# Two more raw weight buffers, one hi and one lo tile fewer, and the first chunk's transposes issued later, in a float32 hybrid layer

## The chip, the cores and the metric

The kernel runs on one core of a Trainium2 chip. The metric is the device time of one execution in microseconds (us). Five engines work in parallel, each in the order of its own queue: TensorE (PE) with its weight loads (PEld), VectorE (DVE), ScalarE (ACT), GpSimd (POOL) and SyncE (SP). SP issues nearly all of the DMA transfers here.

## The reference, cut to what matters

One decoder layer over 272 positions (16 meta tokens and 256 tokens) with a model width of 2048. The part that the change touches is its feed-forward half, on the 256 tokens:

```python
u = rmsnorm(h, attn_norm_w[l]);  proj = u @ w_in[l]           # 2048 x 7184
# ... differential attention (8 heads) and gated DeltaNet (8 heads) on the columns of proj
h = h + jnp.concatenate([o_a, o_d], axis=-1) @ w_out[l]
u = rmsnorm(h, ffn_norm_w[l])
h = h + (jax.nn.silu(u @ w_gate[l]) * (u @ w_up[l])) @ w_down[l]
return h[:, LEAD:]                                             # the 256 tokens
```

FFN_HIDDEN is 5632. All inputs and outputs are float32.

## The kernel before, in words

**Products in three parts.** A float32 weight tile is split into a high part `hi` (ACT rounds the raw tile, L274) and a low part `lo` (DVE subtracts, L275). The left sides are split likewise (`uh`, `ul`; `hT` has both parts in one tile). A product is hi\*hi, hi\*lo and lo\*hi, three matmuls of 128x512 on PE (L1381 in the stages in question, L1199 before).

**Weights as one stream.** The list `order` holds all transfers in the order of use, 512 KB each: w_in, w_out, then for the first 512 columns of the hidden layer (chunk 0) w_gate and w_up one after the other, then for chunks 1 to 10 (`NCH` is 11) pairs of a gate and an up tile, then w_down in two passes of 1024 output columns, with pairs of tiles. A raw tile goes through three steps:

- `load_to` (L261) issues its transfer into a buffer of the ring `raw`;
- `split_to` makes `hi` and `lo` from it;
- `next_w` hands these to the products, and before that asks for the split of the tiles ahead and for the loads ahead of those.

The rings have `WR` = 4 raw buffers, and `WS` = 4 tiles of `hi` and of `lo`, with `WS2` = 2 more of each once the feed-forward stage has opened a pool of its own (`more`): six.

**Plain pairs and groups.** In chunks 1 to 10 there are 8 pairs of weight tiles each (q = 0 to 7), in a pass of w_down 22. A plain pair is two w tiles of 12 matmuls. At the q in `SEVEN` (2, 4, 6) and `DSEVEN` (7, 9, 11, 13, 15, 17, 19) a pair is multiplied in Strassen's manner, seven products in place of eight: the group has four weight tiles, named by their kinds g (6 matmuls), u (3), t (6) and s (6), 21 in all. g and u come from the two raw tiles; t and s are sums of both, made by DVE (L291 to L294) in a ring of two `sum` buffers when g is split. A raw buffer is free again when the last of these has read it: L275's `lo` of the tile, as a rule.

**Who sets the order.** ACT and SP take their instructions in the order in which the code is written (`PINNED`). PE's and DVE's order is set by a scheduler when the program is built, so it shifts when buffers or steps change. Work beside the products (`tasks`) is written as generators; the products call `tasks.step()` after each part, and a `yield n` resumes after n steps.

**Chunk 0.** Gate and up columns of the first chunk are streamed one after the other (`stream`); `ffn_task` then multiplies them on DVE (L1306, `gact`), and after a `yield` `to_hT` transposes the result on PE (L1277), copies it out on ACT (L1292) and makes its low part on DVE (L1293). At that time PE already works on chunk 1, whose first products are in the other set of PSUM banks (`aux`).

**The down product.** Pass 1 makes columns 0 to 1023, pass 2 the rest; each ends with additions to the residual (L1516) and stores (L1518). The residual comes back by L1484.

Of the kernel before, what the change touches and what calls it, by code (L numbers as in the profile page):

```python
# [8 lines left out]
F32 = mybir.dt.float32  # L9
# [6 lines left out]
P = 128  # L16
# [13 lines left out]
KC = (0, 72, 144, T)  # L30
R1, R2 = 12, 10
WR, WS = 4, 4
WS2 = 2
WHOLE = 8
SEVEN = (2, 4, 6)
DSEVEN = (7, 9, 11, 13, 15, 17, 19)
# [130 lines left out]
def layer(tc, xT, aw, x, w_in, w_ba, w_out, w_gate, w_up, w_down, cmask, dist, par, out):  # L167
# [3 lines left out]
    def pool(name, bufs=1, space=None):  # L171
        cm = tc.tile_pool(name=name, bufs=bufs, **({"space": space} if space else {}))
        return cm, cm.__enter__()
# [8 lines left out]
    cm_w, wp = pool("wp")  # L182
# [21 lines left out]
    def act(out_, in_, func, **kw):  # L204

        act_table("silu_and_others" if func == AF.Silu else "natural_log_exp_and_others")
        S.activation(out_, in_, func, **kw)
# [4 lines left out]
    def at_least(k, n):  # L212
        return lambda: done.get(k, 0) >= n
# [39 lines left out]
    pos = [0, 0, 0, 0]  # L253
    more = []

    def load_to(n, parts=1, eng=nc.sync):
        while pos[0] < min(n, len(order)):
            src, a, b = order[pos[0]]
            raw = wp.tile([P, a, b], F32, tag="raw", bufs=WR, name=f"raw{pos[0]}")
            for i in range(0, a, a // parts):  # L260
                eng.dma_start(out=raw[:, i:i + a // parts], in_=src[:, i:i + a // parts])  # L261
            raws[pos[0]] = raw
            pos[0] += 1

    def split(raw, n, a, b, parts=1, rows=slice(0, None)):

        k = n % (WS + WS2) if more else 0
        if k < WS:
            hi, lo = (wp.tile([P, a, b], F32R, tag=t, bufs=WS, name=f"{t}{n}") for t in ("hi", "lo"))
        else:  # L270
            hi, lo = (more[0].tile([P, a, b], F32R, tag=f"{t}2", bufs=WS2, name=f"{t}{n}") for t in ("hi", "lo"))
        for j in range(0, a, a // parts):
# [5 lines left out]
    def split_to(n, parts=1):  # L278
        while pos[1] < min(n, len(forms)):
            m = pos[1]  # L280
            kind, i = forms[m]
            load_to(i + (1 if kind == "w" else 2))
            src, a, b = order[i]
            if kind == "w":
                ready[m] = split(raws.pop(i), m, a, b, parts)
                pos[3] += 1
            elif kind == "g":
                g, u = raws[i], raws[i + 1]
                ready[m] = split(g, m, a, b)
                t, s = (more[0].tile([P, 2, 512], F32, tag="sum", bufs=2, name=f"{n}{i}") for n in "ts")  # L290
                V.tensor_tensor(t[:, 0], u[:, 0], g[:, 0], ALU.subtract)  # L291
                V.tensor_tensor(t[:, 1], u[:, 1], u[:, 0], ALU.subtract)  # L292
                V.tensor_tensor(s[:, 0], u[:, 1], t[:, 0], ALU.subtract)  # L293
                V.tensor_tensor(s[:, 1], g[:, 1], s[:, 0], ALU.subtract)  # L294
                sums_["t"], sums_["s"] = t, s
            elif kind == "u":
                raws.pop(i)
                ready[m] = split(raws.pop(i + 1), m, a, b, rows=slice(1, 2))
                pos[3] += 2
            else:  # L300
                ready[m] = split(sums_[kind], m, a, b)
            pos[1] += 1

    def next_w():
        i = pos[2]
        pos[2] += 1
        split_to(i + WS + (WS2 if more else 0))
        load_to(pos[3] + WR - 1)
        return ready.pop(i)


# [3 lines left out]
    nc.sync.dma_start(out=xr[0][:, 0:1, :], in_=xT[:, 0:1, :])  # L315
    nc.sync.dma_start(out=aw_sb, in_=aw)
    load_to(1, 2, S)

    act_table("natural_log_exp_and_others")
# [820 lines left out]
    def proj(t0):  # L1140

        tasks.until(lambda: mm.live <= 2)
        acc = [mm.now(), mm.now()]
        n = T - t0
        for q in range(4):
            hi, lo = next_w()
            for k in range(4):
                kt = 4 * q + k
                for c in range(2):
                    cs = slice(c * P, (c + 1) * P)  # L1150
                    for i, (a, b) in enumerate(((hi, xh), (hi, xl), (lo, xh))):
                        PE.matmul(acc[c][:, 0:n], a[:, k, cs], b[:, kt, t0:T],  # L1152
                                  start=(kt == 0 and i == 0), stop=(kt == KT - 1 and i == 2))
                tasks.step()
        return acc
# [29 lines left out]
    def stream(kts, lhs, need=None, acc=None, last=True, ring=mm):  # L1185

        first = acc is None
        if first:
            tasks.until(lambda: ring.live <= 2)
            acc = [ring.now(), ring.now()]  # L1190
        for i, kt in enumerate(kts):
            if i % 2 == 0:
                hi, lo = next_w()
            if need:
                tasks.until(need(kt))
            for b in range(2):
                ah, al = lhs(kt, b)
                for j, (l, r) in enumerate(((ah, hi), (ah, lo), (al, hi))):
                    PE.matmul(acc[b], l, r[:, i % 2, :], start=(first and i == 0 and j == 0),  # L1199
                              stop=(last and i == len(kts) - 1 and j == 2))  # L1200
            tasks.step()
            tasks.step()
        return acc
# [68 lines left out]
    def to_hT(c, b, h_):  # L1272

        ring = rings[c % 2]
        pst = yield from ring.get(4, P)
        for j in range(4):
            PE.transpose(pst[:, j, :], h_[:, P * j:P * (j + 1)], ident)  # L1277
        fpool[1].free()
        yield 1
        if c not in hT:  # L1280
            n = f"hT{c}"
            if c < 4:
                hT[c] = bigp.tile([P, 2, 4, SEQ], F32R, tag="big", name=n)
            elif c < 7:
                hT[c] = keep.tile([P, 2, 4, SEQ], F32R, tag=("v_c", "k_c", "q_c")[c - 4], name=n)
            elif c < WHOLE:
                hT[c] = fpool[0].tile([P, 2, 4, SEQ], F32R, tag=n, name=n)
            else:
                hT[c] = fpool[0].tile([P, 4, SEQ], F32, tag=n, name=n)
        bs = slice(P * b, P * (b + 1))  # L1290
        if c < WHOLE:
            S.copy(hT[c][:, 0, :, bs], pst)  # L1292
            V.tensor_tensor(hT[c][:, 1, :, bs], pst, hT[c][:, 0, :, bs], ALU.subtract)  # L1293
        else:
            S.copy(hT[c][:, :, bs], pst)
        ring.free()
        mark(f"hT{c}")

    def ffn_task(c, b, pg, pu):
        g_ = yield from fpool[1].get(512)  # L1300
        act(g_, pg, AF.Silu, scale=rr[:, b:b + 1])
        mm.free()
        yield at_least(f"up{c}", 1)
        yield 1
        ps = pu[b]
        V.scalar_tensor_tensor(g_, ps, rr[:, b:b + 1], g_, ALU.mult, ALU.mult)  # L1306
        mm.free()
        yield 2
        yield from to_hT(c, b, g_)


# [55 lines left out]
    def block(c, name, nq, seven, lhs, need, mid, end):  # L1367
# [15 lines left out]
        for q in range(nq):  # L1383
            k = 2 * q
            if need:
                tasks.until(need(k))
            if q not in seven:
                for col in range(2):
                    hi, lo = next_w()
                    for i in range(2):  # L1390
                        for b in range(2):
                            product(("x", 2 * col + b), lhs(k + i, b), (hi[:, i], lo[:, i]))
                            tasks.step()
                    if q == nq - 1:
                        end(col, x)
                continue
            if not y:
                tasks.until(lambda: other.live == 0)
                y += [other.now() for _ in range(4)]
            tasks.until(at_least(f"side{(name, q)}", 1))  # L1400
            s1, s2_, s3, s4 = sides[name, q]
            plan = (((("y", 0), lhs(k, 0), 0), (("x", 0), lhs(k + 1, 0), 1)), ((("x", 2), s4, 1),),
                    ((("y", 3), s1, 0), (("y", 2), s3, 1)), ((("y", 1), s2_, 0), (("x", 1), lhs(k + 1, 1), 1)))
            for part in plan:
                hi, lo = next_w()
                for bank, a, i in part:
                    product(bank, a, (hi[:, i], lo[:, i]))
                    tasks.step()
            if q == seven[-1]:
                mid(y)  # L1410
# [32 lines left out]
    for b in range(2):  # L1443
        tasks.spawn(ffn_task(0, b, pg[b], pu), urgent=True)
# [180 lines left out]
```

## Time and profile before

| | |
|---|---|
| median of 3 runs | 1223.23 us (1222.27 to 1226.79) |
| profiled execution | 1224.38 us, of which the trace's span is 1222.6 us |
| PE busy | 1209.2 us, 7316 matmuls |
| DVE, ACT busy | 983.6 and 692.3 us |
| DMA | 228.54 MB, mean 187 GB/s, 57.4% of the 16 engines' time on the queue of SP |
| granted TensorE clock | 1.00 |

Times within the span: chunk 0's up columns end at about 557 us, chunks 1 to 10 run to 984.2, pass 1 of the down product to 1099.1, pass 2 to 1218. A matmul of 128x512 has a duration of 0.39 us in the trace, but the next one starts 0.227 us after it, since they are pipelined. So PE is lost only where two starts lie further apart, and its busy share is near 100% even where it barely keeps up.

### The profile page before, as it was taken

The numbers are of one execution on the slowest core, as the hardware profiler recorded it, in microseconds if no ns is written. First come the engines' busy times: TensorE is split into PE (matmuls) and PEld (weight loads), VectorE is DVE, ScalarE is ACT, GpSimd is POOL, SyncE is SP. The second block draws the span as 40 slices with busy tenths as digits, with TensorE's granted clock in tenths as the row PEclk, the third lists the DMA queues.
The fourth block names the chain that finished last, engine by engine and source line by source line (L and its number), as shares of the span: only waits on it lengthen the run. The fifth ranks groups of instructions, "written<-read, shape, count | busy, mean of one in ns | idle before, by whom it ended". The sixth has DMA issues, their size and how long they took to land.

```text
span 1222.6 us, 19223 instructions
## 1 busy us (share of the span) xinstructions
PE 1209.2 (99%) x7316; PEld 1060.0 (87%) x7316; DVE 983.6 (80%) x1573; ACT 692.3 (57%) x1087; POOL 6.1 (0%) x14
## 2 busy tenths in 40 slices
PE   9999999999999999999999999999999999999998
PEld 7999999999999988887888888888888888888876
DVE  7989974686676666668889988998998899886686
ACT  7674465275776665455555556555555665553552
POOL 0000000000000000000000000000000000000000
PEclk9999999999999999999999999999999999999999
DMA  8466564344544645685665665566566565567543
GB/s 293 124 207 195 145 187 121 112 124 145 172 140 139 229 162 178 191 277 167 196 206 186 195 218 190 192 204 217 166 208 216 187 211 197 201 225 276 181 164 133
DMA packets 151869, 228.54 MB, mean 187 GB/s; under 512 B 11736, under 2 KB 72672, under 8 KB 151264
## 3 DMA queue, kind: packets, MB, share of 16 engines
q1 hardware_dynamic: 151232, 226.78, 57.4%
q8 instruction: 57, 0.93, 0.3%
q10 hardware_dynamic: 544, 0.52, 0.1%
q14 instruction: 36, 0.29, 0.1%
HBM read 221.83 MB, written 5.45 MB: 186 GB/s over the span
## 4 chain that ended last, share of the span: by engine, by line
PE 85%; DVE 7%; DMA 4%; ACT 2%; issue 1%; SPq 0%; DVEq 0%; ACTq 0%
PE aux L1381 25%; PE mm L1152 23%; PE mm L1381 21%; PE mm L1199 10%; DVE lo L275 3%; DMA raw<-in_w_down_dram 3%; ACT hi L274 1%; PE aux L1100 1%; PE aux L1055 1%; DMA raw<-in_w_in_dram 0%; PE mm L1277 0%; DVE s L293 0%; DMA raw<-in_w_up_dram 0%; DVE r L581 0%; PE aux L1277 0%
## 5 line engine op out<-in xcount | busy, mean ns | idle before, releaser
L274 ACT CAST hi<-raw 128x1024 fp32r<-128x1024 f32 (+1 forms) x412 | 405.1, 996 | 325.0 <-PE mm L1152 93.3
L275 DVE TENSOR_TENSOR lo<-raw,hi 128x1024 fp32r<-128x1024 f32 (+1 forms) x412 | 470.6, 1153 | 141.6 <-ACT hi L274 139.1
L1152 PE MATMUL mm<-xh,hi 128*128 128x272 f32 (+2 forms) x896 | 258.4, 289 | 0.0
L1152 PE MATMUL mm<-xl,hi 128*128 128x272 f32 (+2 forms) x896 | 255.9, 286 | 0.9 <-DVE xl L384 0.6
L1152 PE MATMUL mm<-xh,lo 128*128 128x272 f32 (+2 forms) x896 | 255.0, 286 | 1.0 <-DVE lo L275 1.0
L1152 PEld LDWEIGHTS mm<-xl,hi 128*128 128x128 f32 x896 | 168.5, 188 | 2.2 <-DVE xl L384 2.0
L1152 PEld LDWEIGHTS mm<-xh,hi 128*128 128x128 f32 x896 | 168.6, 188 | 2.1 <-issue 1.5
L1152 PEld LDWEIGHTS mm<-xh,lo 128*128 128x128 f32 x896 | 168.2, 188 | 1.6 <-DVE lo L275 1.4
L1381 PE MATMUL aux<-hi,uh 128*128 128x512 f32 x260 | 101.6, 391 | 0.0
L1381 PE MATMUL mm<-hi,uh 128*128 128x512 f32 x260 | 101.6, 391 | 0.0
L1381 PE MATMUL aux<-hi,ul 128*128 128x512 f32 x260 | 101.3, 390 | 0.0
L1381 PE MATMUL mm<-hi,ul 128*128 128x512 f32 x260 | 101.2, 389 | 0.0
L1381 PE MATMUL aux<-lo,uh 128*128 128x512 f32 x260 | 101.2, 389 | 0.0
L1381 PE MATMUL mm<-lo,uh 128*128 128x512 f32 x260 | 101.2, 389 | 0.0
L1381 PE MATMUL aux<-hi,hT 128*128 128x512 f32 x216 | 70.2, 389 | 0.0
L1381 PE MATMUL mm<-hi,hT 128*128 128x512 f32 x216 | 70.0, 389 | 0.0
L274 ACT CAST hi<-s 128x1024 fp32r<-128x1024 f32 x44 | 46.3, 1053 | 38.0 <-DVE s L294 34.5
L291 DVE TENSOR_TENSOR t<-raw,raw 128x512 f32<-128x512 f32 x44 | 30.2, 687 | 38.7 <-DMA raw<-in_w_down_dram 25.2
L274 ACT CAST hi<-t 128x1024 fp32r<-128x1024 f32 x44 | 46.3, 1053 | 26.2 <-DVE t L292 11.3
L1381 PEld LDWEIGHTS aux<-hi,ul 128*128 128x128 f32 x260 | 48.8, 188 | 10.2
L1381 PEld LDWEIGHTS mm<-hi,ul 128*128 128x128 f32 x260 | 48.8, 188 | 10.2
L1381 PEld LDWEIGHTS mm<-hi,uh 128*128 128x128 f32 x260 | 48.8, 188 | 10.0
(418 smaller groups left out, 2046.8 us busy)
## 6 DMA issues: line engine op xcount, KB each, us to landing
raw<-in_w_in_dram SPq DMA_DIRECT2D x111, 512.0 KB, 3.6
raw<-in_w_gate_dram SPq DMA_DIRECT2D x88, 512.0 KB, 3.7
raw<-in_w_up_dram SPq DMA_DIRECT2D x88, 512.0 KB, 4.4
raw<-in_w_down_dram SPq DMA_DIRECT2D x88, 512.0 KB, 4.6
raw<-in_w_out_dram SPq DMA_DIRECT2D x32, 512.0 KB, 4.2
x<-x1d SPq DMA_DIRECT2D x8, 256.0 KB, 4.8
xr<-in_xT_dram SPq DMA_DIRECT2D x7, 272.0 KB, 5.8
out_dram<-x SPq DMA_DIRECT2D x6, 256.0 KB, 5.1
```

The source lines that it names most:

```text
L274: S.copy(hi[:, js], raw[:, js])
L275: V.tensor_tensor(lo[:, js], raw[:, js], hi[:, js], ALU.subtract)
L291: V.tensor_tensor(t[:, 0], u[:, 0], g[:, 0], ALU.subtract)
L1055: PE.matmul(pss[m][:, cut[n]], q[ms, P * n:P * (n + 1)], k[ms, 0:NK[n]], start=True, stop=True)
L1100: PE.matmul(po[:, n, :], l, r, start=(j == 0), stop=(j == 1 + n))
L1152: PE.matmul(acc[c][:, 0:n], a[:, k, cs], b[:, kt, t0:T], start=(kt == 0 and i == 0), stop=(kt == KT - 1 and i == 2))
L1199: PE.matmul(acc[b], l, r[:, i % 2, :], start=(first and i == 0 and j == 0), stop=(last and i == len(kts) - 1 and j == 2))
L1381: PE.matmul((x if bank[0] == "x" else y)[bank[1]], l, r, start=first, stop=todo[bank] == 0)
```

## The change

The raw ring gets two more buffers, from the pool of the feed-forward stage, so six raws can be loaded or waiting. The rings of `hi` and `lo` lose one tile each there, so five tiles can be ahead of PE and not six. Bytes of SBUF stay the same: two raw tiles of 512 KB come, one `hi` and one `lo` of 512 KB go. And `ffn_task`, which runs for chunk 0 alone, waits eight steps and not two between the multiplication and the transposes.

```diff
-WS2 = 2
+WS2, WR2 = 1, 2
...
     def load_to(n, parts=1, eng=nc.sync):
         while pos[0] < min(n, len(order)):
             src, a, b = order[pos[0]]
-            raw = wp.tile([P, a, b], F32, tag="raw", bufs=WR, name=f"raw{pos[0]}")
+            if more and pos[0] % (WR + WR2) >= WR:
+                raw = more[0].tile([P, a, b], F32, tag="raw2", bufs=WR2, name=f"raw{pos[0]}")
+            else:
+                raw = wp.tile([P, a, b], F32, tag="raw", bufs=WR, name=f"raw{pos[0]}")
...
         split_to(i + WS + (WS2 if more else 0))
-        load_to(pos[3] + WR - 1)
+        load_to(pos[3] + WR + (WR2 if more else 0) - 1)
...
     def ffn_task(c, b, pg, pu):
...
-        yield 2
+        yield 8
         yield from to_hT(c, b, g_)
```

Lines after L259 move by three in the changed kernel: L275 becomes L278, L291 L294, L1277 L1280, L1306 L1309, L1381 L1384.

What stands on PE at the end of chunk 0, before; `aux` are products of chunk 1, and `mm<-ident,gact` are the transposes, four in a row for each half of the tokens:

```order
L1381 MATMUL aux_6787<-hi_6674,uh 128x512
L1381 MATMUL aux_6787<-lo_6675,uh 128x512
L1381 MATMUL aux_6787<-hi_6674,ul 128x512
L1277 MATMUL mm_6813<-ident,gact_6609 128x128 x4
L1381 MATMUL aux_6788<-hi_6674,uh 128x512
L1381 MATMUL aux_6788<-lo_6675,uh 128x512
L1277 MATMUL mm_6818<-ident,gact_6612 128x128 x4
L1381 MATMUL aux_6788<-hi_6674,ul 128x512
```

And now, from the same product (`hi` 6674 is 6690 here):

```order
L1384 MATMUL aux_6781<-hi_6690,ul 128x512
L1384 MATMUL aux_6782<-hi_6690,uh 128x512
L1384 MATMUL aux_6782<-lo_6691,uh 128x512
L1384 MATMUL aux_6782<-hi_6690,ul 128x512
L1384 MATMUL aux_6779<-hi_6714,uh 128x512
L1384 MATMUL aux_6779<-lo_6715,uh 128x512
L1384 MATMUL aux_6779<-hi_6714,ul 128x512
L1384 MATMUL aux_6780<-hi_6714,uh 128x512
L1384 MATMUL aux_6780<-lo_6715,uh 128x512
L1384 MATMUL aux_6780<-hi_6714,ul 128x512
L1280 MATMUL mm_6841<-ident,gact_6607 128x128 x4
L1280 MATMUL mm_6846<-ident,gact_6610 128x128 x4
```

The first four transposes have moved behind nine more products, and the second four stand directly behind them.

What stands on DVE in pass 2 of the down product, before, from the t tile of one group to the u tile of the next. The number in a name (`raw394`, `lo473`) counts raw and split tiles through the program: 472 and 473 are the t and s of a group, 474 and 475 the plain pair behind it, 476 and 477 the g and u of the next group, and t394 and s394 that group's sums:

```order
L275 TENSOR_TENSOR lo472_11875<-t390_11851,hi472_11874 128x1024
L275 TENSOR_TENSOR lo473_11885<-s390_11852,hi473_11884 128x1024
L275 TENSOR_TENSOR lo474_11901<-raw392_11839,hi474_11900 128x1024
L291 TENSOR_TENSOR t394_11934<-raw395_11904,raw394_11866 128x512
L292 TENSOR_TENSOR t394_11934<-raw395_11904 128x512
L293 TENSOR_TENSOR s394_11935<-raw395_11904,t394_11934 128x512
L275 TENSOR_TENSOR lo475_11919<-raw393_11864,hi475_11918 128x1024
L294 TENSOR_TENSOR s394_11935<-raw394_11866,s394_11935 128x512
L275 TENSOR_TENSOR lo476_11931<-raw394_11866,hi476_11930 128x1024
L275 TENSOR_TENSOR lo477_11944<-raw395_11904,hi477_11943 128x512
```

And now, in the same place:

```order
L278 TENSOR_TENSOR lo472_11885<-t390_11858,hi472_11884 128x1024
L294 TENSOR_TENSOR t394_11941<-raw395_11874,raw394_11849 128x512
L295 TENSOR_TENSOR t394_11941<-raw395_11874 128x512
L278 TENSOR_TENSOR lo473_11901<-s390_11859,hi473_11900 128x1024
L296 TENSOR_TENSOR s394_11942<-raw395_11874,t394_11941 128x512
L297 TENSOR_TENSOR s394_11942<-raw394_11849,s394_11942 128x512
L278 TENSOR_TENSOR lo474_11917<-raw392_11793,hi474_11916 128x1024
L278 TENSOR_TENSOR lo475_11929<-raw393_11837,hi475_11928 128x1024
L278 TENSOR_TENSOR lo476_11938<-raw394_11849,hi476_11937 128x1024
L278 TENSOR_TENSOR lo477_11954<-raw395_11874,hi477_11953 128x512
```

The sums t394 and s394, which read raw395, the last raw tile of the next group, have moved ahead of `lo` of s (473) and of both plain tiles (474, 475). With four raws, raw395 takes the buffer of raw391; with six, that of raw389. In pass 1 DVE's order changes in the same way from the sums of the group at q = 13 on; those of q = 9 and 11 stay behind `lo` of their g tile.

## The prediction

> **What bounds the kernel now.** I read the engines' shares first, then the busy time by stage, then what ended PE's idle time, then the chain of waits where PE stalls.
>
> ```profile
> PE 1209.2 (99%) x7316; PEld 1060.0 (87%) x7316; DVE 983.6 (80%) x1573; ACT 692.3 (57%) x1087; POOL 6.1 (0%) x14
> ```
>
> PE is busy in all but 13.4 of 1222.6 us, and the change removes no matmul. So it can give back only idle time of PE in the stages that it touches: chunk 0's end, chunks 1 to 10, and the two passes of the down product.
>
> ```profile
> 555.00:600.00 45.00, 43.66 (x198) 35.87 (x197) 39.38 (x56) 24.36 (x29) 0.00 (x0) 1.00 0.54 173
> 600.00:984.20 384.20, 384.20 (x1733) 318.84 (x1732) 347.84 (x414) 219.01 (x244) 0.00 (x0) 1.00 0.61 199
> 984.20:1099.10 114.90, 114.90 (x513) 95.22 (x512) 106.26 (x152) 66.55 (x80) 0.00 (x0) 1.00 0.61 206
> 1099.10:1218.00 118.90, 115.64 (x508) 94.73 (x506) 85.47 (x98) 52.71 (x54) 0.00 (x0) 1.00 0.56 190
> ```
>
> The columns are the stretch, its length, then busy time of PE, weight loads, DVE, ACT and POOL, the granted clock (1.00 throughout), DMA share and GB/s. PE loses 1.34 us at chunk 0's end and 3.3 us in down pass 2 (from 1099.1); in the chunks and in pass 1 it loses nothing. DVE, at 347.84 of 384.20 us, is nearly as full as PE.
>
> The loss at chunk 0, on PE and then on DVE:
>
> ```profile
> 562.36 0.39 PE L1381 MATMUL aux<-hi,ul 128*128 128x512 f32 x1
> 564.08 0.66 PE L1277 MATMUL mm<-ident,gact 128*128 128x128 f32 x4 [1.34 <-DVE gact L1306]
> ```
>
> ```profile
> 563.29 0.74 DVE L1306 SCALAR_TENSOR_TENSOR gact<-mm,rr,gact 128x512 f32<-128x512 f32 x1
> ...
> 564.15 0.74 DVE L1306 SCALAR_TENSOR_TENSOR gact<-mm,rr,gact 128x512 f32<-128x512 f32 x1
> ```
>
> The transposes stand 1.72 us behind the matmul before them, because DVE writes gact late. The loss in pass 2, by periods of one plain pair of weight tiles and one Strassen-like group (12 + 12 + 21 = 45 matmuls), L1381's matmuls only:
>
> ```profile
> 1157.57:1167.77 10.20, 10.20 (x46) 8.45 (x45) 1.00 0.54 191
> 1167.77:1178.84 11.07, 10.54 (x47) 8.37 (x45) 1.00 0.53 176
> 1178.84:1190.27 11.43, 10.50 (x46) 8.37 (x45) 1.00 0.53 183
> 1190.27:1202.57 12.30, 10.51 (x46) 8.37 (x45) 1.00 0.53 174
> ```
>
> An undisturbed period is 10.20 us, 0.2267 per matmul: 2.72 for a plain tile, 4.76 for a group. The last three exceed it by 0.87 + 1.23 + 2.10 = 4.2 us. The chain of waits there:
>
> ```profile
> 1166.62 6.34 DMA raw<-in_w_down_dram
> ...
> 1178.48 5.95 DMA raw<-in_w_down_dram
> ...
> 1189.95 6.77 DMA raw<-in_w_down_dram
> ```
>
> These starts are 11.86 and 11.47 us apart: a loop of load and DVE, longer than PE's period, uses up the lead and then stalls PE. DVE in one turn of it:
>
> ```profile
> 1173.09 0.69 DVE L291 TENSOR_TENSOR t<-raw,raw 128x512 f32<-128x512 f32 x1 [3.08 <-DMA raw<-in_w_down_dram]
> 1173.69 0.68 DVE L292 TENSOR_TENSOR t<-raw 128x512 f32<-128x512 f32 x1
> 1174.30 0.69 DVE L293 TENSOR_TENSOR s<-raw,t 128x512 f32<-128x512 f32 x1
> 1174.90 1.22 DVE L275 TENSOR_TENSOR lo<-raw,hi 128x1024 fp32r<-128x1024 f32 x1
> 1176.04 0.68 DVE L294 TENSOR_TENSOR s<-raw,s 128x512 f32<-128x512 f32 x1
> 1176.64 1.82 DVE L275 TENSOR_TENSOR lo<-raw,hi 128x1024 fp32r<-128x1024 f32 x2
> 1178.38 1.22 DVE L275 TENSOR_TENSOR lo<-t,hi 128x1024 fp32r<-128x1024 f32 x1
> ```
>
> The first sum t of the next group waits 3.08 us for its second raw tile (u), and the lo that PE wants next stands behind it in DVE's queue (1174.90). That u could only be requested when lo of the old u had freed its buffer, 4 raws back.
>
> **The change part by part.**
>
> *Transposes.* They move behind 9 more matmuls, to 562.36 + 10 x 0.2267 = 564.6. The first gact is done at 563.29 + 0.74 = 564.03, the second at 564.89, when the second four come up (four take some 0.45 in a row, by the 0.66 of the row above less one's drain: about 565.05). Both fit even with DVE unmoved, and DVE's new order puts the gact ahead of one lo (1.13). Removed: 1.72 - 0.23 = 1.5 us. The copies out of the transposes come about 2 us later against PE's work; the next products in those banks come 18 matmuls on, 4.1 us. Bounds: 0 (the wait moves along) to -1.5; I take -1.5.
>
> *Six raws.* They remove no load and add none. u's buffer is now that of the raw six earlier, the second plain tile of the pair before, so the request can leave half a period sooner. But DVE's new order in the deep part of both passes uses that up: t of the next group now stands ahead of lo of s of this group. One turn becomes: t, t, lo s, s, s, lo of plain tile a, lo of plain tile b; b's end frees u's buffer. By the pitches above (0.60 for a sum, 1.13 for a lo, 1.22 for the last) a's lo ends 0.6 + 0.6 + 1.13 + 0.6 + 0.6 + 1.22 = 4.8 after t starts, and b's 1.15 later. Then u is the second load of a burst of four. What a second load takes, bounded by the nearest rows:
>
> ```profile
> 1139.87 0.37 SPq L261 DMA_DIRECT2D raw<-in_w_down_dram  x1
> 1141.00 0.37 SPq L261 DMA_DIRECT2D raw<-in_w_down_dram  x1
> 1026.39 0.37 SPq L261 DMA_DIRECT2D raw<-in_w_down_dram  x1
> 1027.53 0.37 SPq L261 DMA_DIRECT2D raw<-in_w_down_dram  x1
> 1177.88 0.37 SPq L261 DMA_DIRECT2D raw<-in_w_down_dram  x1
> ```
>
> ```profile
> raw<-in_w_down_dram SPq DMA_DIRECT2D x1, 512.0 KB, 3.6
> raw<-in_w_down_dram SPq DMA_DIRECT2D x1, 512.0 KB, 6.2
> raw<-in_w_down_dram SPq DMA_DIRECT2D x1, 512.0 KB, 3.5
> raw<-in_w_down_dram SPq DMA_DIRECT2D x1, 512.0 KB, 5.0
> raw<-in_w_down_dram SPq DMA_DIRECT2D x1, 512.0 KB, 5.2
> ```
>
> The second fence has the us to landing, in the same order: firsts of a burst 3.6 and 3.5, their seconds 6.2 and 5.0, and 5.2 for the second of another burst. The burst at 1139.87 is spaced as the new one will be and has the 6.2; 1027.53 also came 1.14 after a first and has 5.0. I take their middle, 5.6. The new turn is L = 4.8 + 1.15 + 5.6 = 11.5 us (10.95 to 12.15): no shorter than the 11.5 to 11.9 of now, and above 10.20.
>
> *Rings of five.* A cast waits until PE has left the tile five back:
>
> ```profile
> 676.62 1.05 ACT L274 CAST hi<-raw 128x1024 fp32r<-128x1024 f32 x1 [1.67 <-PE aux L1381]
> ```
>
> Cast 1.05, lo 1.22 and two handovers make 2.5 us from PE's release to a finished lo (about 0.2 for the handovers is my estimate). The tightest tile is the plain one behind a group: between its release and its use PE has only the group's 4.76 us, where a sixth tile gave 2.72 more. Its slack falls from 5.0 to 2.3 us.
>
> *Pass 2*, counted from its start: PE has 7 plain pairs ahead (38.1 us), so lo of tile a of q8 is done at 38.1 + 2.5 = 40.6; from there one turn per group, five turns to a of q18: 40.6 + 5 L = 98.1. PE wants it at 12 pairs and 6 groups, 65.3 + 28.6 = 93.9, and its lo one matmul later, 94.1. Lost: 4.0 us (1.3 to 7.3), against 4.2 now: -0.2.
>
> *Pass 1*: DVE keeps the old order for the first three groups, whose raws come early; the new one begins behind group 11. Tile a of q12 is done at 9 pairs + 2 groups + 2.5 = 61.0; three turns later, 61.0 + 3 L = 95.5 against 94.1: +1.4 us (0 to 3.4), where nothing is lost now.
>
> *Chunks.* Only one t per chunk (that of q6) has the late request, and pairs 7, 0 and 1 follow, in which DVE catches up. Slack 2.3 less 11.5 - 10.2 leaves 1.0: no cost taken; where L exceeds 12.5, the excess in each of ten chunks.
>
> The moved x1 loads and output stores (two raws now stand ahead of the x1 loads on SP) fall in the plain pairs that open a pass, with 7 pairs of work in hand: nothing.
>
> Sum: -1.5 - 0.2 + 1.4 = -0.3 us. The profiled execution took 1224.38 us (span 1222.6), 1.15 above the median of 1223.23; the difference is set against the median: 1222.9, say 1223.0.
>
> **The rivals.**
>
> *B, the loads keep ahead.* If the second load landed 4.3 us after its request, L would be 10.25 and all stalls would go: -1.5 - 4.2 = -5.7, 1217.5. For it speaks a close pair in the chunks, whose second load landed after 4.3 us:
>
> ```profile
> 661.50 0.37 SPq L261 DMA_DIRECT2D raw<-in_w_gate_dram  x1
> 662.10 0.37 SPq L261 DMA_DIRECT2D raw<-in_w_up_dram  x1
> ```
>
> ```profile
> raw<-in_w_up_dram SPq DMA_DIRECT2D x1, 512.0 KB, 4.3
> ```
>
> The two are 0.6 us apart. Against it stand the three seconds of the down product. The Trainium skill, SBUF — State Buffer, "The DMA setup-cost knee", prices a transfer at about 2 us plus its bytes over 436 GB/s, which makes an estimate of 3.2 us here; by that L would be 9.2 and the outcome this rival's. The trace agrees for a first load (3.6) and not for a second.
>
> *C, the shallower rings and the late load decide.* If a second load takes 6.4 us or more, L is 12.4: pass 1 loses 61.0 + 37.2 - 94.1 = 4.1, pass 2 40.6 + 62.0 - 94.1 = 8.5, together with the transposes -1.5 + 4.1 + 8.5 - 4.2 = +6.9: 1230. From there each chunk adds its excess too. The row of 6.2 is near; 5.0 and 5.2 are not.
>
> *D, only the transposes fail*: the gact moves back with them, and the sum is +1.2: 1224.5.
>
> **How the numbers follow.** 0.5% is 6.1 us, about what a measurement can tell from no change: 1217.1 to 1229.3 is "same". My forecast has 0.64 (own range 1218.5 to 1228.3, from L = 10.95: -1.5 - 2.9 + 0 = -4.4, and L = 12.15: -1.5 + 3.1 + 3.4 = +5.0). B 0.18, of which 0.04 beyond 1217.1; C 0.10, of which 0.08 above 1229.3; D 0.08. Faster 0.04, same 0.88, slower 0.08. The range takes in B and the upper end of L: 1217.5 to 1228.5.
>
> **What would show it.** No gap before L1280's transposes in chunk 0. In both passes t (L294) idles for a raw of w_down and lo of s stands behind it; turns of 11 to 12 us; PE gaps of 0.5 to 1.5 us at lo of plain tile a of q14 to q18, in pass 1 as well. ACT's waits on PE grow in the chunks while PE keeps its 100%. I am wrong if a second load lands in under 4.5 us (no gaps) or over 6.4 (gaps in the chunks), or if DVE's queue runs so far ahead that t's wait falls before anything is due.

## The result

The changed kernel takes 1229.28 us (median of 7 runs, 1228.21 to 1230.45), the kernel before, run beside it, 1224.82 us (7 runs, 1222.27 to 1226.79). The ratio is 1.0042 (95% interval 1.0032 to 1.0052): slower by about 4.5 us. The forecast was 1223.0, a gain of 0.3 us within a range of 1217.5 to 1228.5.

The same four stretches as before, in the changed kernel's profile (execution 1228.59 us, span 1226.8): chunk 0's end, chunks 1 to 10, pass 1, pass 2. The columns are those of the prediction's table; the second row begins at the first matmul of chunk 1 and overlaps the first.

```profile
555.00:600.00 45.00, 45.00 (x204) 37.33 (x203) 40.07 (x57) 25.89 (x33) 0.00 (x0) 1.00 0.55 180
559.30:983.20 423.90, 423.90 (x1911) 351.92 (x1911) 382.46 (x459) 242.65 (x272) 0.00 (x0) 1.00 0.60 197
983.20:1102.10 118.90, 116.98 (x516) 95.70 (x515) 108.19 (x154) 66.09 (x79) 0.00 (x0) 1.00 0.61 207
1102.10:1222.60 120.50, 116.99 (x508) 94.46 (x506) 86.77 (x98) 53.57 (x55) 0.00 (x0) 1.00 0.53 181
```

From 555 us up to pass 1 PE is idle nowhere: the gap at chunk 0 is gone, and the chunks lose nothing. Both passes now lose time, pass 1 too, which was full before. What PE waited for in the two passes (us in total, times, longest):

```profile
PE mm L1384 <- DVE lo L278: 3.4, 5, 0.9
PE aux L1384 <- DVE lo L278: 2.1, 3, 0.9
```

All of it is `lo`. These 5.5 us are counted from the trace's ends of the matmuls; by the starts, the two passes are 8.5 us longer than the shortest that any run here showed (118.88 and 120.51 against 115.83 and 115.08). PE's gaps in pass 2 stand at these matmuls, the last bracket being the idle time ahead of each:

```profile
1166.12 0.50 PE L1384 MATMUL mm<-lo,hT 128*128 128x512 f32 x1 [0.39 <-DVE lo L278]
1177.83 0.50 PE L1384 MATMUL mm<-lo,hT 128*128 128x512 f32 x1 [0.93 <-DVE lo L278]
1189.39 0.50 PE L1384 MATMUL mm<-lo,hT_hl 128*128 128x512 f32 x1 [0.93 <-DVE lo L278]
1198.88 0.50 PE L1384 MATMUL aux<-lo,rest 128*128 128x512 f32 x1 [0.34 <-DVE lo L278]
1201.46 0.50 PE L1384 MATMUL mm<-lo,hT_hl 128*128 128x512 f32 x1 [0.93 <-DVE lo L278]
```

Four are `lo` of plain tile a of q12, q14, q16 and q18, and 1198.88 is `lo` of an s. One turn on DVE there:

```profile
1161.05 0.69 DVE L294 TENSOR_TENSOR t<-raw,raw 128x512 f32<-128x512 f32 x1 [2.40 <-DMA raw<-in_w_down_dram]
1161.65 0.69 DVE L295 TENSOR_TENSOR t<-raw 128x512 f32<-128x512 f32 x1
1162.26 1.22 DVE L278 TENSOR_TENSOR lo<-s,hi 128x1024 fp32r<-128x1024 f32 x1
1163.51 0.69 DVE L296 TENSOR_TENSOR s<-raw,t 128x512 f32<-128x512 f32 x1
1164.23 0.69 DVE L297 TENSOR_TENSOR s<-raw,s 128x512 f32<-128x512 f32 x1
1164.84 4.09 DVE L278 TENSOR_TENSOR lo<-raw,hi 128x1024 fp32r<-128x1024 f32 x4
1168.85 1.22 DVE L278 TENSOR_TENSOR lo<-t,hi 128x1024 fp32r<-128x1024 f32 x1
1172.76 0.69 DVE L294 TENSOR_TENSOR t<-raw,raw 128x512 f32<-128x512 f32 x1 [2.69 <-DMA raw<-in_w_down_dram]
```

DVE stands idle for 2.69 us ahead of t, and the `lo` of s and those of the plain tiles, which PE wants next, are queued behind it. t waits for a load that could be issued only when `lo` of plain tile b, the second of the four from 1164.84, had ended. The chain of waits, by start, length and holder, shows that load and the next:

```profile
1164.84 2.36 DVE lo L278 x2
1167.21 0.02 issue
1167.22 5.41 DMA raw<-in_w_down_dram
...
1178.94 5.26 DMA raw<-in_w_down_dram
...
1190.50 5.77 DMA raw<-in_w_down_dram
```

A turn is 1172.76 - 1161.05 = 11.71 us, against PE's 10.20.

**By stage, in all profiles taken of the two kernels.** Each number is from the first matmul of a stage to the first of the next (pass 2: to the end of its last), in us; the rows marked "again" are the second and third profiles described under the experiments.

| kernel | up to w_out | chunks 1 to 10 | pass 1 | pass 2 | span |
|---|---|---|---|---|---|
| before | 411.5 | 425.44 | 115.83 | 119.28 | 1222.6 |
| before, again | 413.8 | 424.41 | 115.83 | 118.29 | 1222.9 |
| after | 413.1 | 423.88 | 118.88 | 120.51 | 1226.8 |
| after, again | 413.5 | 423.88 | 118.94 | 120.22 | 1227.8 |
| after, once more | 411.5 | 423.88 | 119.77 | 121.91 | 1227.8 |

The stages left out (start, w_out, chunk 0, tail) agree within 0.9 us. The first column is 411.5 in one profile of each kernel and 413.1 to 413.8 in the others, so this step is not of the change. The means of the others: chunks 424.93 to 423.88, -1.05; pass 1 115.83 to 119.20, +3.4; pass 2 118.79 to 120.88, +2.1. Together +4.4 us, near the 4.46 between the medians. Pass 1 is the firm part: it was 115.83 in both profiles of before. Pass 2 of before differs by 1 us between two profiles, so its +2.1 is less certain.

The shortest that any run here showed, 423.88, 115.83 and 115.08, is taken below as undisturbed.

### The profile page after: what moved, and what is told of

Same layout as the page of the kernel before. It is cut to its first block, busy times and chain, and to the rows that moved or that the text cites. A ratio compares the mean times of both kernels' runs of the same rounds, so it can differ in the third digit from the quotient of the medians.

```text
span 1226.8 us, 19226 instructions
## 1 busy us (share of the span) xinstructions
PE 1211.0 (99%) x7316; PEld 1059.6 (86%) x7316; DVE 985.2 (80%) x1573; ACT 692.1 (56%) x1087; POOL 6.0 (0%) x14
## 4 chain that ended last, share of the span: by engine, by line
PE 84%; DVE 8%; DMA 4%; ACT 2%; issue 2%; SPq 0%; DVEq 0%; ACTq 0%
PE mm L1384 23%; PE aux L1384 22%; PE mm L1155 21%; PE mm L1202 11%; DVE lo L278 4%; DMA raw<-in_w_down_dram 3%; ACT hi L277 1%; PE aux L1103 1%; DVE r L584 1%; PE aux L1058 1%; DVE t L294 0%; DMA raw<-in_w_in_dram 0%; DVE s L296 0%; PE mm L1280 0%; DVE t L295 0%
## 5 line engine op out<-in xcount | busy, mean ns | idle before, releaser
L278 DVE TENSOR_TENSOR lo<-raw,hi 128x1024 fp32r<-128x1024 f32 (+1 forms) x412 | 465.9, 1155 | 132.5 <-ACT hi L277 129.1
L1384 PE MATMUL aux<-hi,uh 128*128 128x512 f32 x260 | 101.6, 391 | 0.0
L1384 PE MATMUL mm<-hi,uh 128*128 128x512 f32 x260 | 101.6, 391 | 0.0
L1384 PE MATMUL aux<-hi,ul 128*128 128x512 f32 x260 | 101.2, 389 | 0.0
L1384 PE MATMUL mm<-hi,ul 128*128 128x512 f32 x260 | 101.2, 389 | 0.0
L1384 PE MATMUL aux<-lo,uh 128*128 128x512 f32 x260 | 101.2, 389 | 0.0
L1384 PE MATMUL mm<-lo,uh 128*128 128x512 f32 x260 | 101.2, 389 | 0.0
L1384 PE MATMUL aux<-hi,hT 128*128 128x512 f32 x216 | 70.1, 390 | 0.0
L1384 PE MATMUL mm<-hi,hT 128*128 128x512 f32 x216 | 70.0, 389 | 0.0
L278 DVE TENSOR_TENSOR lo<-s,hi 128x1024 fp32r<-128x1024 f32 x44 | 53.7, 1222 | 13.9 <-ACT hi L277 13.7
L1384 PEld LDWEIGHTS aux<-hi,ul 128*128 128x128 f32 x260 | 48.8, 188 | 10.2
L1384 PEld LDWEIGHTS mm<-hi,ul 128*128 128x128 f32 x260 | 48.8, 188 | 10.2
L1384 PEld LDWEIGHTS aux<-lo,uh 128*128 128x128 f32 x260 | 48.8, 188 | 10.0
```

The costliest lines, as they stand in the source:

```text
L278: V.tensor_tensor(lo[:, js], raw[:, js], hi[:, js], ALU.subtract)
L1384: PE.matmul((x if bank[0] == "x" else y)[bank[1]], l, r, start=first, stop=todo[bank] == 0)
```

## The experiments

Theory L, from the prediction: a loop of DVE and a late load sets the passes, because t of the next group waits in DVE's queue ahead of work that PE wants. Its rivals: the shallower rings of `hi` and `lo` do it; or the loads alone are too slow, whatever the order.

**1. The transposes alone.** The kernel before, with the later transposes only.

```diff
-        yield 2
+        yield 8
```

> The kernel before with the later transposes of chunk 0 alone (yield 8; rings and raws as before). My theory: the 1.5 us gap of TensorE in front of these transposes goes and nothing else changes, so 1.5 us less than the kernel before, ratio 0.9988, and the stalls at the end of down pass 2 stay at about 4.2 us. Rival (the wait moves along with the transposes): ratio 1.000 with a gap of 1.3 us at the new place.

Measured: 1223.48 us (12 runs) against 1224.18 (27 runs of before), 0.9990 (0.9978 to 1.0003). The chunks took 424.23 us, pass 1 115.83, as in before. PE has no wait for gact left, at the old place or a new one, so the rival is out. Pass 2 took 121.75 in this profile, with the same late loop as in before: it varies. The chunks became about 0.7 us shorter on average, less than the 1.5 expected; the interval of the total contains 1, so the time alone does not show it.

**2. The rings alone.** The kernel before, with five tiles of `hi` and `lo` and still four raws.

```diff
-WS2 = 2
+WS2 = 1
```

> The kernel before with hi and lo rings of five alone (four raws, yield 2). Theory L (the loss comes from the loop of load and DVE that is longer than TensorE's 10.2 us period, and a ring of five starts it with one plain tile, 2.7 us, less in hand): pass 2 of the down product loses about 2.7 us more than the 4.2 of before, pass 1 0.5 to 1.5, the chunks nothing: 3 to 4 us slower, ratio 1.0025 to 1.0035. Rival R (the six raws do the harm, by bursts of four loads or by moving the sums ahead in VectorE's queue, and the rings nothing): ratio 1.000, losses as before.

Measured: 1227.12 us (12 runs), 1.0019 (1.0007 to 1.0030): the rings cost 2 to 3 us by themselves, a little under the 1.0025 to 1.0035 expected, which the interval reaches, and clear of the rival's 1.000. The profiled execution was the fastest of these runs (1223.2), with chunks 425.77, pass 1 116.33 and pass 2 116.69, and shows too little of it. Pass 1's 0.5 us is one gap at the first group's `lo`; it is there in every kernel with rings of five and the sums on DVE. A second profile shows where more can be lost:

> Rings of five alone, run again for a second profile. The first profile's execution was 1223.2 us, its other runs 1226 to 1228, so the first pass 2 (116.69 us) was a lucky one: I expect pass 1 again at 116.3 and pass 2 at 119 to 121 now. If instead pass 2 is near 116.7 again, the time of the other runs lies ahead of the feed-forward half and not in the rings.

That execution took 1231.24 us, more than any of the twelve before it: chunks 428.73, pass 1 116.37, pass 2 120.04. What PE waited for from chunk 0's end on:

```profile
PE mm L1381 <- DVE lo L275: 4.9, 5, 2.2
PE mm L1277 <- DVE gact L1306: 1.2, 1, 1.2
PE mm L1277 <- DVE gact L1362: 1.0, 1, 1.0
```

Pass 1 and pass 2 came as this second forecast said. But pass 2, with 116.69 and 120.04 in the two profiles against 119.28 and 118.29 of before, does not show the 2.7 us more that the first one expected. The chunks, of which nothing was expected, lost time too: besides the gap at chunk 0 (L1306), the next chunk's transposes were late as well (L1362). The chain of waits through that place goes back to a load of 6.59 us that began 31 us earlier:

```profile
625.23 6.59 DMA raw<-in_w_up_dram
```

So with four raws and rings of five a slow load can reach PE even in the chunks; it did in one of two profiles. With six raws none did in the three profiles of the changed kernel, nor in experiments 4 and 7: 423.88 each.

**3. Rings and raws together, without the later transposes.** The changed kernel with the old `yield`.

```diff
-        yield 8
+        yield 2
```

> The changed kernel with the transposes of chunk 0 at their old place (yield 2; six raws, rings of five). Theory: 1.3 to 1.5 us slower than the changed kernel, ratio to before 1.0052 to 1.0055, the gap of 1.3 us in front of the transposes back. Rival (with two more raws VectorE reaches the gact earlier, so the transposes would not wait at their old place either): same time as the changed kernel, ratio 1.0042, no gap.

Measured: 1230.28 us (6 runs), 1.0049 (1.0030 to 1.0068); chunks 425.07, pass 1 119.13, pass 2 122.04. The 1.2 us in the chunks are the transposes, with a wait for gact again; the total (1.0049) cannot tell the 1.0052 to 1.0055 expected from the rival's 1.0042. Against rings alone the two raws bring pass 1 from 116.3 to 119.1: this part is theirs, and experiment 4 shows that it is the order on DVE that comes with them. The intervals of the two totals touch, so this rests on the stage and not on the total.

**4. The order alone.** The changed kernel, but the two sums in buffers of their own that swap with each group: the next t is written where this group's s stood, so the scheduler has to put it behind the `lo` of that s. Six raws, rings of five, loads and arithmetic are as in the changed kernel.

```diff
+    swap = [0]
...
-                t, s = (more[0].tile([P, 2, 512], F32, tag="sum", bufs=2, name=f"{n}{i}") for n in "ts")
+                swap[0] ^= 1
+                t, s = (more[0].tile([P, 2, 512], F32, tag=f"sum{k ^ swap[0]}", bufs=1, name=f"{n}{i}") for k, n in enumerate("ts"))
```

> The changed kernel with one thing more: the sums t and s have a buffer each of their own, and the next group's t takes the buffer of this group's s. So t of the next group must stand behind lo of s in VectorE's queue, no longer in front of it; six raws, rings of five, yield 8, loads and their number stay. Theory L: from the start of t to the request of the next u it is then 4.2 us and not 6.1, a turn is about 9.7 to 10.0 us, below TensorE's 10.2, and the stalls of both passes of the down product nearly vanish (under 1 us of 8): 1217.5 to 1220 by the earlier runs of before, ratio 0.995 to 0.997. Rival R2 (the bursts of four loads, or the smaller lead of five tiles, make the stalls whatever VectorE's order is): within 1 us of the changed kernel, ratio 1.003 to 1.005.

Measured: 1220.38 us (10 runs), 0.9966 (0.9955 to 0.9978): faster than before, and 8.9 us below the changed kernel's median. The rival's range, 1.003 to 1.005, is out. Chunks 423.88, pass 1 116.36, pass 2 115.08. PE's only wait for weights from chunk 0 on is the gap at the first group, and DVE runs at PE's period:

```profile
PE mm L1386 <- DVE lo L279: 0.2, 1, 0.2
```

```profile
1155.78 1.22 DVE L279 TENSOR_TENSOR lo<-s,hi 128x1024 fp32r<-128x1024 f32 x1 [1.30 <-ACT hi L278]
1157.04 0.69 DVE L296 TENSOR_TENSOR t<-raw,raw 128x512 f32<-128x512 f32 x1
...
1158.85 3.49 DVE L279 TENSOR_TENSOR lo<-raw,hi 128x1024 fp32r<-128x1024 f32 x3
...
1167.24 0.69 DVE L296 TENSOR_TENSOR t<-raw,raw 128x512 f32<-128x512 f32 x1
```

From t to t is 10.20 us, and t has no wait for a load. The loads are no faster: the second load of the burst that starts at 1160.10, issued 1.14 later, landed 5.4 us after its issue, as in the changed kernel. What became shorter is DVE's part of the loop, from t to the end of `lo` of b: 4.2 us here (1157.04 to about 1161.2) instead of 6.16 there (1161.05 to 1167.21), since `lo` of s and a sum have left it. 4.2 + 5.4 + 0.1 = 9.7 us is under PE's period, 6.16 + 5.41 + 0.14 = 11.71 above it. This refutes the rival that the loads are too slow as such, and that rings of five must lose in the passes beyond the 0.5 us.

**5. The same order with four raws and rings of six.** The kernel before with `yield 8` and the separate sum buffers of experiment 4.

> The kernel before with the later transposes and with the separate buffers of the sums (t of the next group takes the buffer of this group's s), four raws and rings of six. Theory L: with four raws, u is requested only after lo of the old u, and t already stood behind lo of s, so the turn stays 11 to 11.5 us and pass 2 keeps its stalls of 4 to 7 us: as the later transposes alone, ratio 0.998 to 1.000. So the gain of the kernel with both would need the six raws. Rival (the separate buffers alone bring the gain): ratio 0.996 to 0.997, no stalls in pass 2.

Measured: 1222.10 us (12 runs), 0.9988 (0.9979 to 0.9996). Chunks 424.16, pass 1 115.83, pass 2 116.99 with one gap at `lo`. In pass 2 t still waits for its load:

```profile
1158.70 0.69 DVE L293 TENSOR_TENSOR t<-raw,raw 128x512 f32<-128x512 f32 x1 [2.26 <-DMA raw<-in_w_down_dram]
```

From t to t it is still 11.1 to 11.9 us there, longer than PE's 10.20 and near the 11 to 11.5 expected; the loss of pass 2 in this profile, 1.9 us, is less than the 4 to 7 expected. The total is 0.12% below before, and experiment 1 had 0.10% from the later transposes alone. So with four raws the separate sum buffers give nothing that these intervals show, and the rival (0.996 to 0.997 from the buffers alone) is out. The two belong together: six raws let the load leave earlier, and the order keeps DVE from spending that lead.

**6. The sums on GpSimd.** The changed kernel, with t and s made by POOL, so that no `lo` can stand behind a waiting t.

```diff
-                V.tensor_tensor(t[:, 0], u[:, 0], g[:, 0], ALU.subtract)
+                G.tensor_tensor(t[:, 0], u[:, 0], g[:, 0], ALU.subtract)
...
```

(All four sums, L294 to L297.)

> The changed kernel with the four sums of each group (t, s) computed on GpSimd, idle there, in place of VectorE; six raws, rings of five, bursts of loads and the late request of u stay. Theory L: the harm is that VectorE's queue stands behind t while t waits for its load, so with t in another queue lo of s and of the plain tiles no longer wait: the stalls of the down passes go, about 1217 to 1220, ratio 0.995 to 0.997, unless GpSimd needs over 2.5 us for one sum (then a group's four sums take more than a period and GpSimd itself is late: ratio over 1.01, and TensorE then waits for lo of t and s and not of the plain tile). Rival R2 (the late load itself is what TensorE waits for): stalls as in the changed kernel, ratio 1.003 to 1.005.

Measured: 1226.59 us (6 runs; before 1223.52 of 19), 1.0030 (1.0018 to 1.0043). Pass 2 took 115.08, as theory L says: no stall with t out of the queue. Pass 1 lost 6.4 us (122.25), which it does not say. Some 3.5 us of that stand just ahead of the first group and in it, where PE waits three times between 1019 and 1027 us; the rest comes in periods of 10.67 us instead of 10.20. A sum costs more in this kernel, and DVE's `lo` beside it too (groups of the page: busy, mean ns of one, idle before):

```profile
L278 DVE TENSOR_TENSOR lo<-raw,hi 128x1024 fp32r<-128x1024 f32 (+1 forms) x412 | 569.0, 1407 | 151.1 <-ACT hi L277 147.1
...
L294 POOL TENSOR_TENSOR t<-raw,raw 128x512 f32<-128x512 f32 x44 | 71.5, 1624 | 707.1 <-PE mm L1202 384.4
...
L296 POOL TENSOR_TENSOR s<-raw,t 128x512 f32<-128x512 f32 x44 | 89.4, 2031 | 1.2 <-DVE lo L278 1.2
```

A sum takes 1.6 to 2.0 us instead of 0.69, the same `lo` on average 1407 ns, where the changed kernel's page has

```profile
L278 DVE TENSOR_TENSOR lo<-raw,hi 128x1024 fp32r<-128x1024 f32 (+1 forms) x412 | 465.9, 1155 | 132.5 <-ACT hi L277 129.1
```

So this run only half counts for the theory: in pass 2 the stalls go with t out of DVE's queue, but the change brings a bound of its own, DVE and POOL slowing each other (the last section has the rows). That this sets all of pass 1's loss is argued and not shown.

**7. A second queue for the loads.** The changed kernel, with every second load of w_down issued by GpSimd and the rest by SP: if SP's queue holds the second load back, this shortens it.

```diff
+            q = nc.gpsimd if pos[0] >= len(order) - 88 and pos[0] % 2 else eng
...
-                eng.dma_start(out=raw[:, i:i + a // parts], in_=src[:, i:i + a // parts])
+                q.dma_start(out=raw[:, i:i + a // parts], in_=src[:, i:i + a // parts])
```

> The changed kernel with every second load of w_down (the b tile of a plain pair and u of a group) issued by GpSimd in place of SyncE, so u is no longer the second load in SyncE's queue; VectorE's order, bytes and rings stay. This separates what the 5.6 us of the second load are. Theory L with the delay made by the queue of one issuing engine: u lands 3.5 to 4.5 us after its request, a turn is about 10.2 us and the stalls of 8 us fall under 2: ratio 0.997 to 0.999. Theory L with the delay made by the shared DMA engines (the Trainium skill, DMA: Bandwidth & Descriptors, "Issuing engines are not separate DMA queues", says that all queues run on the same 16 engines): u lands as late as before, stalls and time as in the changed kernel, ratio 1.003 to 1.005.

Measured: 1246.11 us (4 runs), 1.0184 (1.0170 to 1.0199); pass 1 123.24, pass 2 132.56. GpSimd's loads have a median of 6.7 us, SP's of 4.9:

```profile
raw<-in_w_down_dram SPq DMA_DIRECT2D x44, 512.0 KB, 4.9
raw<-in_w_down_dram POOLq DMA_DIRECT2D x44, 512.0 KB, 6.7
```

These medians do not compare the issuers alone, since GpSimd has the second load of each pair and SP the first. By place in the burst, GpSimd's second loads landed 7.0 to 8.1 us after their issue in pass 2's loop, where SP's took mostly 5.2 to 5.8 in the changed kernel. Neither forecast came true: the load of u landed neither sooner nor as late as before, but later. The run serves as a larger dose instead. The turn on DVE:

```profile
1169.95 0.69 DVE L295 TENSOR_TENSOR t<-raw,raw 128x512 f32<-128x512 f32 x1 [4.62 <-DMA raw<-in_w_down_dram]
...
1184.32 0.69 DVE L295 TENSOR_TENSOR t<-raw,raw 128x512 f32<-128x512 f32 x1 [5.35 <-DMA raw<-in_w_down_dram]
```

It is 14.37 us long, and DVE's total wait of t for loads in pass 2, over the three kernels with six raws (the experiment, the changed kernel, experiment 4):

```profile
DVE t L295 <- DMA raw<-in_w_down_dram: 30.0, 7, 5.6
```

```profile
DVE t L294 <- DMA raw<-in_w_down_dram: 14.2, 6, 3.0
```

```profile
DVE t L296 <- DMA raw<-in_w_down_dram: 3.0, 1, 3.0
```

goes with a loss in pass 2 of 17.5, 5.4 and 0 us. The Trainium skill, DMA: Bandwidth & Descriptors, says in its table of specifications that a DMA issued by GpSimd has a first-byte latency of about 1 us where SP's has 0.6. The sign agrees here for the second loads of a burst, but the difference, 1.2 us or more, is larger than that. The bursts are spaced otherwise too: the second load leaves 1.4 us after the first instead of 1.1, and the third 0.9 us after the second. So the cause of the later landing stays open.

**8. The two kernels again.** Second and third profiles, to see which losses repeat.

> The changed kernel, run again for a second profile: which part of its loss repeats. If the loop of load and DVE sets it, pass 1 is again 118.5 to 119.5 us long (115.83 undisturbed) and chunks 1 to 10 again 423.9; pass 2 between 119.5 and 122.5 (115.08 undisturbed), with PE's gaps again at lo of plain tiles and DVE idle before t (L294) for a raw of w_down. The 1.9 us wait of PE before w_out (L733, for r of L712), in which the changed kernel's profile differed too, is not of the change and does not come back: that stage is then near 411.5 us. The rival says that stage belongs to the change: then it is near 413 again.

> As for the second profile of the changed kernel: a third one, with the same numbers expected.

> The kernel before, run again for a second profile. Chunks 1 to 10 again about 425.4 us (the transposes' gap), pass 1 again 115.83, pass 2 anywhere from 116.5 to 122, since its stalls followed the loads' landings in each run so far (119.28 in the first profile). If pass 2 of before were steady, it would be 119.3 again.

Measured: the changed kernel 1229.62 and 1229.61 us, the kernel before 1224.69 (and 1221.10 in one more run beside them); the stages stand in the table of the result. The chunks and both passes of the changed kernel repeat, pass 1 once a little above the expected 119.5 (119.77). The stage up to w_out was 413.5 and 411.5 us, so the 411.5 expected came once, and 413.8 in the kernel before. So its step of 2 us (PE's wait of 1.7 to 1.9 us at L733, L730 in the kernel before) comes and goes in both kernels. The chunks of before came out at 424.41, not 425.4: the gap at the transposes is 0.2 to 1.3 us of PE's waits, not a fixed amount.

```profile
PE mm L1277 <- DVE gact L1306: 0.2, 1, 0.2
```

**Not tried.** Six raws with rings of six do not fit in the memory left to that pool, so the raws alone, with the old rings, have no run.

## Why the prediction was wrong

The mechanism was right, and the terms that failed are the two of the down product: pass 1, forecast at +1.4 us, and pass 2, forecast at -0.2. The runs showed +3.4 and +2.1, because the late loop starts later in pass 1 than was reckoned, each turn is longer than 11.5 us, and pass 2 of the kernel before loses less than its one profile showed.

*What bounds the kernel, and the mechanism: right.* PE waits for `lo`, `lo` stands behind t in DVE's queue, t waits for the second load of a burst. The place was right as well: tile a's `lo` of q8 in pass 2 was to end at 40.6 us after the pass's start and ended at 1142.69 - 1102.10 = 40.59.

*Transposes, -1.5: right in mechanism, too large.* No gap is left, but the old gap is not the same in every run; the mean of the profiles gives -1.05, and the totals of experiment 1 -0.7, which is within their noise.

*The turn, L = 11.5: 11.7 to 12.0.* From the t at about 1149 to the one at about 1197, four turns, it was 11.69, 11.65 and 12.03 us on average in the three profiles. By parts in the turn shown: t to the end of a's `lo` 5.01 (I had 4.8; the pitches left out the two small gaps around L296 and L297), b's `lo` 1.15, load 5.41, handover 0.14. My 5.6 for the load was fair: the loads of this kind in the loop of pass 2 took 5.2 to 5.8 us, and once 6.9.

*Pass 2, -0.2: measured +2.1.* The step that failed is the difference of two small numbers, each many turns of the loop. From `lo` of a in q8 (1142.69) to that in q18 (1201.42) five turns took 11.74 us each, and by my own formula this gives 40.6 + 5 x 11.74 - 94.1 = 5.2 us lost instead of 4.0, and the three profiles lost 5.4, 5.1 and 6.8. The mean of the three is 1.8 above my 4.0. The other 0.5 is the baseline: I took the one profile's loss of 4.2 us as the kernel's, where a second has 3.2.

*Pass 1, +1.4: measured +3.4.* For the changed kernel itself this is the largest miss. I let the late loop begin with tile a of q12 at 61.0 us, timed by PE's release. PE is 0.75 us later there, with eight transposes early in the pass (115.83 against 115.08); that moves both sides alike. But the rows of DVE show two sums t ahead of that `lo`, and ACT's cast of a (the second fence) waits for PE:

```profile
1042.51 1.23 DVE L278 TENSOR_TENSOR lo<-s,hi 128x1024 fp32r<-128x1024 f32 x1
1043.65 0.69 DVE L294 TENSOR_TENSOR t<-raw,raw 128x512 f32<-128x512 f32 x1
1044.25 0.69 DVE L295 TENSOR_TENSOR t<-raw 128x512 f32<-128x512 f32 x1
1044.86 3.49 DVE L278 TENSOR_TENSOR lo<-raw,hi 128x1024 fp32r<-128x1024 f32 x3
```

```profile
1043.34 1.06 ACT L277 CAST hi<-raw 128x1024 fp32r<-128x1024 f32 x1 [0.86 <-PE aux L1384]
```

The `lo` of a ends at 1044.86 + 1.22 - 983.2 = 62.9, which is 1.9 later than reckoned, or about 1.2 beyond the transposes' 0.75. The cast of a ends at 1044.40, and without the sums its `lo` could have followed at once, so the sums add some 0.4 us. About 0.5 is the first group's gap that comes with rings of five, which makes PE itself late; the rest lies in PE's last matmuls on the tile and the handovers. Three turns of 11.66 on average end at 97.9, where PE wants it at 94.1 + 0.75 = 94.85: 3.05 lost, of which 1.2 is the start and 0.5 the longer turns beyond the 1.4. The prediction left out the gap at the first group and the sums ahead of that `lo`. In experiment 4 the loop starts as late (63.0 us) and pass 1 loses nothing beyond the 0.5, so the late start costs only where the turns are longer than PE's period.

*Rings of five, nothing in the chunks: right for this kernel,* though experiment 2's second profile suggests that it is the raws that keep it so. ACT's waits on PE grew as expected; in the chunks (600 to 983 us) they were 29.5 + 28.5 = 58 us before and 110.6 after, and cost PE nothing:

```profile
ACT hi L274 <- PE aux L1381: 29.5, 37, 1.7
ACT hi L274 <- PE mm L1381: 28.5, 36, 1.7
```

```profile
ACT hi L277 <- PE mm L1384: 61.8, 55, 1.7
ACT hi L277 <- PE aux L1384: 48.8, 43, 1.7
```

In pass 1 the rings cost 0.5 us at the first group, which is part of the later start above.

*The rivals.* C's time (1230) came nearly true, but not by its cause: the loads mostly took 5.2 to 5.8 us and not 6.4, and the chunks lost nothing. B's condition, a loop shorter than PE's period, was met in experiment 4 by the order and not by the load; it gave 1220.4.

*The time.* The terms as measured, -1.05 + 3.4 + 2.1, make +4.4 instead of -0.3. Set against the 1223.23 of the three runs the result seems 6 us off; 1.6 us of that is the baseline, 1224.82 over seven runs. The range was too narrow because it took the uncertainty of the load alone, not that of the loop's start and of the old kernel's stalls.

## What to carry to other kernels

More buffers let a load leave earlier, but a scheduler that sees the data come earlier may put the waiting instruction ahead of ready work on an in-order engine, and then the lead is lost again: trace the loop from the wait round to the request, and add it up against the bound engine's period. Where one such instruction holds up others, look for a buffer whose reuse forces the order (here, t into the place of the last s) before adding more depth. A stall that is a small difference between two periods is multiplied by every turn and varies from run to run: take several profiles of before, and let the range hold the start of the loop as well as its length.

## What the runs showed of the hardware

- Two-input float32 operations on GpSimd and DVE slow each other when both run. POOL's first sum in a group, begun while DVE was idle, took 1.29 us, the next ones beside DVE's `lo` 2.2 to 2.3; four `lo` beside them took 7.90 us together:

```profile
1154.17 1.29 POOL L294 TENSOR_TENSOR t<-raw,raw 128x512 f32<-128x512 f32 x1 [5.80 <-DMA raw<-in_w_down_dram]
1155.42 2.32 POOL L295 TENSOR_TENSOR t<-raw 128x512 f32<-128x512 f32 x1
...
1165.56 7.90 DVE L278 TENSOR_TENSOR lo<-raw,hi 128x1024 fp32r<-128x1024 f32 x4 [0.52 <-ACT hi L277]
```

  With POOL idle four such `lo` take 4.09 us (changed kernel, 1164.84). The Trainium skill, SBUF — State Buffer, "SBUF: two separate sides", says that DVE operations with two SBUF inputs and GpSimd operations that read SBUF hold one pair of ports in turn, each for a whole instruction. The numbers agree: one sum and one `lo` by themselves are 1.2 + 1.1 = 2.3 us, about the time that each took beside the other.
- A 512 KB load that follows another by 1.1 us landed 5.2 to 5.8 us after its issue in the loop of the changed kernel's pass 2, with one of 6.9 in the three profiles, where the first of a burst took 3.5 to 4.0. In experiment 7's loop, where GpSimd issued the second load, it took 7.0 to 8.1 us.
